# In front of the MLP: eight modulation steps instead of six, and the first quarter's residual rows made by ScalarE and GpSimd

## The chip, the core and the metric

The kernel runs on one core of one Trainium2 chip. The metric is the device time of one launch in microseconds (us); lower is better. The figure for a kernel is the median of its runs.

## What is computed

One step of one layer of a decoder trunk, for 256 prompt tokens and 8 sample tokens, with 2048 channels, all in float32. Only the part around the change matters here:

```
mod = silu(c) @ w_ada + b_ada                     # 2048 x (6*2048)
sh1, sc1, gt1, sh2, sc2, gt2 = split(mod, 6)
...                                               # three mixers -> merged
out = merged @ w_out
x   = x + gt1 * rmsnorm(out, g_post_mix)          # first residual
h2  = rmsnorm(x, g_pre_mlp) * (1 + sc2) + sh2
y2  = square(relu(h2 @ w_mlp_up)) @ w_mlp_down    # 2048 -> 8192 -> 2048
x   = x + gt2 * rmsnorm(y2, g_post_mlp)
```

## The kernel before, in words

Activations stand transposed: 128 channels in the partitions, 264 tokens (256 + 8) in the row. A weight block of 128x128 is stationary, the tokens move. Float32 accuracy is kept with three products per weight block: weights and activations are split into a high and a low part ("whi"/"wlo" for weights), and lines 671, 672 and 673 multiply high by high, high by low and low by high. A *granule* is 4x256 or 2x512 weights, read by one SyncE load into a "raw" buffer; ScalarE writes the high part (line 631), VectorE the low part (line 113). There are buffers for three granules of split weights, so the splits run up to three granules ahead of TensorE, and each split waits for TensorE to give a buffer back.

The output projection (`w_out`) is eight blocks of 256 channels, m = 0 to 7, four granules each. Behind each block `gated` makes the squares (line 1461) and the gated values g (VectorE line 1464, ScalarE line 1467), and adds the squares to `sqacc` (line 110). One granule into the next block, TensorE turns g round to token rows (line 893). Then `block_rows` takes products on VectorE (line 1482), copies the rows into the tiles `og` (ScalarE line 1489, VectorE line 1490) and takes squares on ScalarE (line 1486). g lies in a tile "gt", of which there are two; g of a block can be written only when the squares of the block two before it are through.

The last of the six modulation vectors (gt2) isn't needed until the end of the MLP. It is made in 16 *steps*, k = 0 to 15; a step loads two tiles of 128x1024 from `w_ada` (line 346) and does four matmuls (line 383). `pre.load` loads the first six steps during the output projection, and `rounds.steps(n)` puts n of them into TensorE's program at three places in front of the MLP: two behind the last block, one behind the transposes of the last g, three behind the sums for the sample tokens. The other ten are done inside the MLP, in five batches of two.

In front of the MLP stands a chain of small work. The row norm r1 comes out of `sqacc` (lines 1505, 1506 and 235 to 240); the norm r2 of the new x is worked out from sums without making the new x first (lines 1561 to 1581). Then `quad(q)` makes, for a quarter of the channels, x transposed and scaled by r2: a matmul of x1 with a diagonal matrix `dg` that holds r2 (line 1617). For the first quarter x1 isn't updated yet, so a second matmul adds og times a diagonal of r1*r2 (line 1619; `d1` holds r1). `put_quad` scales, shifts and splits the result (VectorE line 1629, ScalarE line 1631, splits at lines 113 and 116). `residual(q)` makes x1 + og*r1 for a quarter on VectorE (line 1597); `begin_up` runs the first 512 columns of the up projection with quads 1 to 3 and residuals 2, 3 and, last, 0 in between.

Tiles named `b` all come from one pool of 28 (`NBLK`): 128 partitions by 1056 floats. In the output projection these are the merged activations in two parts (8 tiles), x1 (4), og (4; the two for the second half of the channels are first written at block 4) and the loaded steps (2 each).

Who orders what: in the output projection only TensorE's order is the one written; a scheduler orders the other engines and gives out the tiles when the program is built. From `rounds.steps(2)` to the end of `begin_up` TensorE, VectorE and ScalarE have the written order. Every engine runs its list strictly in order.

Of the kernel before, what the change touches and what calls it, by code (L numbers as in the profile page):

```python
# [10 lines left out]
AF = mybir.ActivationFunctionType  # L11
ALU = mybir.AluOpType
# [3 lines left out]
P = 128  # L16
D = 2048
KT = D // P
# [25 lines left out]
RATES = ((1.8, 0.5), (1.6, 0.5), (1.25, 0.5), (1.0, 0.5))  # L44
ST_BUFS = 4
VB_BUFS = 2
N_PRE = 6
PRE_AT = (2, 3, 4)
ADA_BATCH = 4
ADA_LEAD = 3  # L50
PAIRED = 72
# [13 lines left out]
def hybrid_step_kernel(  # L65
# [9 lines left out]
    V, S, T = nc.vector, nc.scalar, nc.tensor  # L75
# [13 lines left out]
    def nm(s):  # L89
        uid[0] += 1  # L90
        return f"{s}_{uid[0]}"

    def blk(shape=None, dt=F32):
        shape = shape or [P, 4, NT]
        return blkp.tile(shape, dt, tag="b", name=nm("b"))

    def sm(shape=None):
        return psm.tile(shape or [P, 512], F32, tag="sm", name=nm("sm"))

    def tmp(shape, tag, bufs=2):  # L100
        return tp.tile(shape, F32, tag=tag, name=nm(tag), bufs=bufs)
# [17 lines left out]
    def apart(v):  # L119
        return v.rearrange("p n (r c) -> p n r c", r=2)  # L120

    def by_two(v):
        return v.rearrange("p n (c r) -> p n r c", r=2)
# [15 lines left out]
    ident, ones, triu = cst[:, 0:128], cst[:, 128:256], cst[:, 256:384]  # L139
# [91 lines left out]
    def rstd_sqrt(ms, scale, out):  # L231

        n, w = out.shape
        xx, aa = tmp([P, 16], "sx")[0:n, 0:w], tmp([P, 16], "sa")[0:n, 0:w]
        S.activation(out, ms, AF.Sqrt, scale=scale, bias=eps)
        V.tensor_scalar(xx, ms, scale, EPS, ALU.mult, ALU.add)
        V.reciprocal(out, out)
        mul(aa, out, out)
        V.scalar_tensor_tensor(aa, aa, -0.5, xx, ALU.mult, ALU.mult)
        V.scalar_tensor_tensor(out, aa, 1.5, out, ALU.add, ALU.mult)  # L240
# [154 lines left out]
    rounds = Rounds()  # L395
# [343 lines left out]
    def new_acc():  # L739
        return pmm.tile([P, 2, 512], F32, tag="mm", name=nm("mm"))  # L740

    def linear(w, k0, nk, c0, width, xh, xl):

        acc = new_acc()
        kc = min(nk, 1024 // width)
        for kb in range(0, nk, kc):
            granule(w, k0, kc, c0, width, [acc], xh, xl, kb, kb == 0, kb + kc == nk)
            background()
        return acc[:, 0:width // P, 0:NT]
# [698 lines left out]
    x1 = [[blk([P, 1024]) for _ in range(2)] for _ in range(2)]  # L1448
# [6 lines left out]
    def gated(m, src, Gv):  # L1455

        k = 2 * m
        sq = tmp([P, 2, NT], "vt")
        g = tmp([P, 2, NT], "gt")
        if m < 7:  # L1460
            S.activation(sq, src, AF.Square)
        else:
            S.activation(sq[:, 0, :], src[:, 0, :], AF.Square)
        V.tensor_scalar(g[:, 1, 0:NP], src[:, 1, 0:NP], Gv[:, k + 1, 0:1], None, ALU.mult)
        if m == 7:
            S.activation(sq[:, 1, :], src[:, 1, :], AF.Square)
        S.activation(g[:, 0, 0:NP], src[:, 0, 0:NP], AF.Copy, scale=Gv[:, k, 0:1])
        if m == 0:
            add(sqacc, sq[:, 0, :], sq[:, 1, :])
        else:  # L1470
            add(sqacc, sqacc, sq[:, 0, :])
            add(sqacc, sqacc, sq[:, 1, :])
        mul(gs[:, k:k + 2, :], src[:, :, NP:NT], Gv[:, k:k + 2, 1:NC])
        return g
# [17 lines left out]
    def block_rows(m, g):  # L1492

        pt = to_tokens(g)
        for t in range(2):
            products(m, t, g, pt)
        put_rows(m, pt, og)
        for t in range(2):
            squares(m, t, g, pt)

    def norms():

        ps = sm([P, 2 + NS])
        for t in range(2):
            T.matmul(ps[:, t:t + 1], sqacc[:, t * P:(t + 1) * P], ones[:, 0:1], start=True, stop=True)
        T.matmul(ps[:, 2:2 + NS], ones, sqacc[:, NP:NT], start=True, stop=True)
        r = tmp([P, 2 + NS], "nr", 1)
        rstd_sqrt(ps, 1.0 / D, r)
        return r
# [3 lines left out]
    og = [[blk([P, 1024]) for _ in range(2)] for _ in range(2)]  # L1513
# [3 lines left out]
    pre = Rounds()  # L1517
    pre.todo = [(5, k) for k in range(KT)]
    for m in range(8):
        if m in PRE_AT:  # L1520
            n = N_PRE // len(PRE_AT)
            for _ in range(n):
                pre.load(True)
        z = linear(w_out[0], 0, KT, m * CW, CW, mH, mL)
        if m < 7:
            g = gated(m, z, G1)
            later.append((now[0], lambda m=m, g=g: block_rows(m, g)))
        if m == 6:

            S.activation(tmp([P, 1], "srr", 1), sqacc[:, 0:1], AF.Sqrt)  # L1530
    rounds.drain()
    rounds = pre
# [4 lines left out]
    order = tc.manual_schedule(engines={mybir.EngineType.PE, mybir.EngineType.DVE, mybir.EngineType.Activation})  # L1537
    order.__enter__()
    Q = nc.gpsimd
    rounds.steps(2)  # L1540
    g = gated(7, z, G1)

    sp = tmp([P, 2, KT, NS], "os2", 1)
# [2 lines left out]
    r1 = norms()  # L1546
# [13 lines left out]
    both = tmp([P, 2, 2 + NS], "fs")  # L1560
    V.reduce_sum(both[:, :, 2:2 + NS], ps.rearrange("p s k b -> p s b k"), axis=mybir.AxisListType.X)
    V.reduce_sum(both[:, :, 0:2], sums, axis=mybir.AxisListType.X)
    rounds.steps(3)

    d1 = tmp([P, 2, P], "vt")
    for t in range(2):
        S.activation(d1[:, t, :], ident, AF.Copy, scale=r1[:, t:t + 1])
    for t in range(2):
        S.copy(in_rows(og, t, 7), pt[:, t])

    xa = tmp([P, KT, NS], "xsn", 1)
    Q.tensor_tensor(gs, gs, r1[:, 2:2 + NS].unsqueeze(1).to_broadcast([P, KT, NS]), op=ALU.mult)
    Q.tensor_tensor(xsT, xsT, gs, op=ALU.add)
    Q.tensor_tensor(xa, xsT, A2[:, :, 1:NC], op=ALU.mult)

    q = tmp([P, 2 + NS], "rr", 1)
# [4 lines left out]
    V.tensor_scalar(q, q, 0.0, None, ALU.max)  # L1581
    r2 = tmp([P, 2 + NS], "rr0", 1)
    rstd_sqrt(q, 1.0 / D, r2)
    dg = tmp([P, 4, P], "gt")
    for t in range(2):
        V.tensor_scalar(dg[:, t, :], ident, r2[:, t:t + 1], None, ALU.mult)
        S.activation(dg[:, 2 + t, :], d1[:, t, :], AF.Copy, scale=r2[:, t:t + 1])
    Q.tensor_tensor(xa, xa, r2[:, 2:2 + NS].unsqueeze(1).to_broadcast([P, KT, NS]), op=ALU.mult)
    Q.tensor_tensor(xa, xa, B2[:, :, 1:NC], op=ALU.add)
    h2h, h2l = [blk(dt=F32R) for _ in range(4)], [blk(dt=F32R) for _ in range(4)]  # L1590
# [1 line left out]
    def residual(q):  # L1592

        cs = slice(q % 2 * 512, q % 2 * 512 + 512)
        for t in range(2):
            x = x1[t][q // 2][:, cs]
            V.scalar_tensor_tensor(x, og[t][q // 2][:, cs], r1[:, t:t + 1], x, ALU.mult, ALU.add)

    def quad(q):

        hs, ls = (apart(h[q])[:, :, :, NP // 2:NT // 2] for h in (h2h, h2l))
        xq = by_two(xa[:, 4 * q:4 * q + 4, :])
        Q.tensor_copy(hs, xq)
        Q.tensor_tensor(ls, xq, hs.bitcast(F32), op=ALU.subtract)
        for i2 in range(2):
            if q > 0:
                ps = sm([P, 2, NP])
            vt = tmp([P, 2, NT], "vt")
            for i in range(2):
                c0 = q % 2 * 512 + (2 * i2 + i) * P  # L1610
                if q == 0:
                    pk = sm([P, NP])
                else:
                    pk = ps[:, i, :]
                for t in range(2):
                    o = pk[:, t * P:(t + 1) * P]
                    T.matmul(o, x1[t][q // 2][:, c0:c0 + P], dg[:, t, :], start=True, stop=q > 0)  # L1617
                    if q == 0:
                        T.matmul(o, og[t][0][:, c0:c0 + P], dg[:, 2 + t, :], start=False, stop=True)
                if q == 0:  # L1620
                    put_quad(q, i2, i, pk, vt)
            if q > 0:
                for i in range(2):
                    put_quad(q, i2, i, ps[:, i, :], vt)

    def put_quad(q, i2, i, src, vt):
        k = 4 * q + 2 * i2 + i
        if i == 0 and (q == 0 or i2 == 0):
            V.tensor_scalar(vt[:, i, 0:NP], src, A2[:, k, 0:1], B2[:, k, 0:1], ALU.mult, ALU.add)
        else:  # L1630
            S.activation(vt[:, i, 0:NP], src, AF.Identity, scale=A2[:, k, 0:1], bias=B2[:, k, 0:1])
        if q == 0 or i == 1:
            a = i if q == 0 else 0
            js = slice(2 * i2 + a, 2 * i2 + i + 1)
            split_tokens(vt[:, a:i + 1, 0:NP], h2h[q][:, js, :], h2l[q][:, js, :], 0, NP)

    quad(0)
    residual(1)

# [5 lines left out]
    def begin_up():  # L1645

        accs = [new_acc(), new_acc()]
        for k in range(0, KT, 2):
            granule(w_mlp_up[0], 0, 2, 0, 2 * CW, accs, h2H, h2L, k, k == 0, k + 2 == KT)
            if k % 4 == 0 and k + 4 < KT:  # L1650
                quad(k // 4 + 1)
            elif k + 6 < KT:
                residual(k // 4 + 2)
            elif k + 2 == KT:
                residual(0)
            if k >= 8:
                background()
        return [a[:, :, 0:NT] for a in accs]
# [107 lines left out]
    dg = tmp([P, 2, P], "vt")  # L1766
# [81 lines left out]
```

## Time and profile before

| | |
|---|---|
| median of 3 runs | 1822.57 us (1820.84 to 1825.6) |
| the profiled execution's own time | 1821.44 us |
| its span, first to last instruction | 1819.4 us |
| its mean granted TensorE clock | 0.998 |
| busy: TensorE, VectorE, ScalarE, GpSimd | 98%, 65%, 55%, 8% |
| HBM traffic over the span | 241 GB/s |

Times in the profile are us from the span's start. A group's row gives busy time and mean length; a timeline row gives start, length, engine, line, operation and, in brackets, how long the engine stood idle ahead of it and what ended that. TensorE's matmul rows overlap: a matmul's row is longer than the distance to the next one. The output projection's last block begins at about 1070 us; the MLP's first granule starts at 1093.92 us.

### The profile page before, as it was taken

What the parts mean: (1) busy time and instruction counts of PE and PEld (TensorE: products, weight loads), DVE (VectorE), ACT (ScalarE), POOL (GpSimd) and SP (SyncE); (2) the same over time, 40 slices, a digit from 0 to 9 for tenths busy, and PEclk for the clock granted to TensorE, in tenths of its full rate; (3) what the DMA queues carried; (4) which work ended last, traced back from release to release, by engine and by line L of the source; (5) the groups of instructions that cost most, each with busy time, mean ns of one, the idle gap of its engine ahead of it and who ended that gap; (6) DMA issues with size and microseconds to landing.
All of it is one profiled execution on the core that took longest, in us unless ns stands there. A gap on an engine that the chain in (4) does not pass through costs nothing.

```text
span 1819.4 us, 42092 instructions
## 1 busy us (share of the span) xinstructions
PE 1780.7 (98%) x16970; PEld 1690.5 (93%) x16970; DVE 1179.1 (65%) x2077; ACT 997.2 (55%) x1824; POOL 138.3 (8%) x228
## 2 busy tenths in 40 slices
PE   7999999999999999999999999999999999999998
PEld 5889999989989988989999989999999999999998
DVE  5566668787576686566555667555666666666666
ACT  5344454666756756655445666454554545454544
POOL 4222000111111111210000000000000000000000
PEclk9999999999999999999999999999999999999999
DMA  9997587788788788897978954877666666666663
GB/s 325 379 347 282 196 293 247 218 260 295 230 285 262 228 261 302 274 326 241 305 252 267 330 166 153 251 255 222 196 195 193 196 196 195 198 196 194 195 193 118
DMA packets 330179, 442.05 MB, mean 243 GB/s; under 512 B 14946, under 2 KB 276944, under 8 KB 329984
## 3 DMA queue, kind: packets, MB, share of 16 engines
q1 hardware_dynamic: 311872, 380.52, 64.7%
q0 software_dynamic: 17184, 57.85, 8.9%
q8 instruction: 133, 2.18, 0.5%
q10 hardware_dynamic: 928, 0.99, 0.2%
q14 instruction: 62, 0.51, 0.1%
HBM read 427.60 MB, written 11.70 MB: 241 GB/s over the span
## 4 chain that ended last, share of the span: by engine, by line
PE 83%; issue 3%; DVE 3%; DMA 3%; ACT 1%; POOL 0%; ACTq 0%; DVEq 0%; SPq 0%; POOLq 0%
PE mm L671 25%; PE mm L673 25%; PE mm L672 25%; PE ada L383 3%; DMA vbc<-vs_d 2%; DVE wlo L113 1%; PE ada L315 1%; PE sm L893 1%; DMA raw<-in_w_in_dram 1%; DVE b L113 1%; PE sm L712 0%; ACT whi L631 0%; PE sm L705 0%; DMA araw<-in_w_ada_dram 0%; PE sm L1617 0%
## 5 line engine op out<-in xcount | busy, mean ns | idle before, releaser
L671 PE MATMUL mm<-b,whi 128*128 128x264 f32 x4600 | 1284.5, 279 | 7.5 <-ACT b L116 3.9
L673 PE MATMUL mm<-b,wlo 128*128 128x264 f32 x4600 | 1272.5, 277 | 6.4 <-DVE wlo L113 4.9
L672 PE MATMUL mm<-b,whi 128*128 128x264 f32 x4600 | 1271.3, 276 | 0.7 <-DVE b L113 0.7
L113 DVE TENSOR_TENSOR wlo<-raw,whi 128x512 fp32r<-128x512 f32 x1136 | 768.8, 689 | 430.4 <-ACT whi L631 427.0
L631 ACT CAST whi<-raw 128x512 fp32r<-128x512 f32 x1136 | 689.0, 616 | 628.9 <-DVE wlo L113 318.9
L671 PEld LDWEIGHTS mm<-b,whi 128*128 128x128 f32 x4600 | 870.8, 189 | 48.2 <-issue 24.8
L673 PEld LDWEIGHTS mm<-b,wlo 128*128 128x128 f32 x4600 | 870.8, 189 | 8.6 <-DVE wlo L113 7.0
L672 PEld LDWEIGHTS mm<-b,whi 128*128 128x128 f32 x4600 | 871.1, 189 | 1.3 <-DVE b L113 1.1
L110 DVE TENSOR_TENSOR b<-b,mm 128x528 f32<-128x528 f32 (+1 forms) x137 | 95.6, 699 | 73.4 <-PE mm L673 65.8
L1148 DVE SCALAR_TENSOR_TENSOR st<-vbc,b,st 128x128 f32<-128x128 f32 (+1 forms) x96 | 34.2, 391 | 54.8 <-DMA vbc<-vs_d 49.9
L1146 ACT ACTIVATE st<-st,fs 128x128 f32<-128x128 f32 (+1 forms) x96 | 37.2, 431 | 51.7 <-DMA st<-in_state_hgrn_dram 29.5
L1785 POOL TENSOR_TENSOR gs<-b,G 128x16 f32<-128x16 f32 x1 | 0.2, 222 | 714.1 <-DVE b L110 714.1
L502 POOL DMA_DIRECT2D b<-in_w_ada_dram x64 | 46.3, 726 | 38.4 <-PE ada L315 31.6
L383 PE MATMUL ada<-araw,cT 128*32 128x512 f32 x296 | 40.8, 601 | 0.4 <-DMA araw<-in_w_ada_dram 0.4
L315 PE MATMUL ada<-b,cT 128*32 128x256 f32 (+1 forms) x640 | 35.2, 358 | 2.1 <-DMA b<-in_w_ada_dram 1.9
L107 DVE TENSOR_TENSOR b<-b,b 128x512 f32<-128x512 f32 (+1 forms) x47 | 34.0, 743 | 1.3 <-ACT b L1260 1.1
L1149 POOL DMA_DIRECT2D out_dram<-st x32 | 23.5, 736 | 132.0 <-DVE st L1148 132.0
L315 PEld LDWEIGHTS ada<-b,cT 128*32 128x32 f32 x640 | 18.2, 114 | 14.2 <-DMA b<-in_w_ada_dram 5.6
L383 PE MATMUL ada<-b,cT 128*32 128x512 f32 x216 | 26.2, 593 | 0.0
L113 DVE TENSOR_TENSOR b<-gt,b 128x528 fp32r<-128x528 f32 x32 | 22.8, 712 | 3.2
L113 DVE TENSOR_TENSOR b<-b 128x1024 f32<-128x1024 f32 (+1 forms) x24 | 24.4, 1019 | 0.0
L1671 ACT ACTIVATE b<-vt 128x528 fp32r<-128x528 f32 x32 | 22.9, 714 | 1.0
(366 smaller groups left out, 902.4 us busy)
## 6 DMA issues: line engine op xcount, KB each, us to landing
raw<-in_w_in_dram SPq DMA_DIRECT2D x231, 512.0 KB, 5.0
raw<-in_w_mlp_up_dram SPq DMA_DIRECT2D x128, 512.0 KB, 3.9
raw<-in_w_mlp_down_dram SPq DMA_DIRECT2D x128, 512.0 KB, 3.6
araw<-in_w_ada_dram SPq DMA_DIRECT2D x74, 512.0 KB, 5.7
b<-in_w_ada_dram SPq DMA_DIRECT2D x54, 512.0 KB, 6.4
b<-in_w_ada_dram POOLq DMA_DIRECT2D x48, 512.0 KB, 10.4
raw<-in_w_branch_dram SPq DMA_DIRECT2D x48, 512.0 KB, 4.5
raw<-in_w_out_dram SPq DMA_DIRECT2D x32, 512.0 KB, 4.9
```

Source lines behind the costliest of these rows:

```text
L107: V.tensor_tensor(o, a, b, op=ALU.mult)
L110: V.tensor_tensor(o, a, b, op=ALU.add)
L113: V.tensor_tensor(o, a, b, op=ALU.subtract)
L315: T.matmul(acc[32 * j:32 * j + 32, 0:n], cT[:, k, :], w[:, n * j:n * j + n], start=k == 0, stop=k == KT - 1)
L383: T.matmul(self.acc[32 * j:32 * j + 32, :], cT[:, k, :], ws[j // 2][:, j % 2 * 512:j % 2 * 512 + 512], start=k == 0, stop=k == KT - 1)
L502: queue.dma_start(w[:, i], w1[k * P:(k + 1) * P, :, self.k0 * P:(self.k0 + self.n) * P])
L631: S.copy(hi, raw)
L671: T.matmul(o, a, xh(k + j), start=first and j == 0, stop=False)
L672: T.matmul(o, a, xl(k + j), start=False, stop=False)
L673: T.matmul(o, b, xh(k + j), start=False, stop=last and j == n - 1)
L1146: S.activation(st[:, i, :], st[:, i, :], AF.Copy, scale=fs[:, h0 + i, b:b + 1])
L1148: V.scalar_tensor_tensor(st[:, i, :], v[:, i, :], k[:, h0 + i, NP + b:NP + b + 1], st[:, i, :], ALU.mult, ALU.add)
```

## The change

Eight steps are loaded ahead instead of six: one during block 1, two each during blocks 2 and 3, three during block 4. The one of block 1 goes into the two "araw" buffers, the other seven take 14 tiles of the pool instead of 12. In front of the MLP they stand as 3 + 1 + 4 instead of 2 + 1 + 3. The first quarter of x1 is updated before quad(0): ScalarE writes og*r1 into a tile `ou`, one instruction of 128x512 for each of the two token tiles, and GpSimd adds it to x1. quad(0) then needs one product per tile and row half, like the other quads; `d1`, the second pair of diagonals and the last `residual(0)` go.

```diff
-N_PRE = 6
-PRE_AT = (2, 3, 4)
+PRE_AT = {1: 1, 2: 2, 3: 2, 4: 3}
...
     for m in range(8):
-        if m in PRE_AT:
-            n = N_PRE // len(PRE_AT)
-            for _ in range(n):
-                pre.load(True)
+        for i in range(PRE_AT.get(m, 0)):
+            pre.load(m > 1)
         z = linear(w_out[0], 0, KT, m * CW, CW, mH, mL)
...
-    rounds.steps(2)
+    rounds.steps(3)
     g = gated(7, z, G1)
...
-    rounds.steps(3)
-
-    d1 = tmp([P, 2, P], "vt")
+    rounds.steps(4)
+
+    ou = blk([P, 2, 512])
     for t in range(2):
-        S.activation(d1[:, t, :], ident, AF.Copy, scale=r1[:, t:t + 1])
+        S.activation(ou[:, t, :], og[t][0][:, 0:512], AF.Copy, scale=r1[:, t:t + 1])
     for t in range(2):
         S.copy(in_rows(og, t, 7), pt[:, t])
...
     Q.tensor_tensor(gs, gs, r1[:, 2:2 + NS].unsqueeze(1).to_broadcast([P, KT, NS]), op=ALU.mult)
+    for t in range(2):
+        Q.tensor_tensor(x1[t][0][:, 0:512], x1[t][0][:, 0:512], ou[:, t, :], op=ALU.add)
     Q.tensor_tensor(xsT, xsT, gs, op=ALU.add)
...
-    dg = tmp([P, 4, P], "gt")
-    for t in range(2):
-        V.tensor_scalar(dg[:, t, :], ident, r2[:, t:t + 1], None, ALU.mult)
-        S.activation(dg[:, 2 + t, :], d1[:, t, :], AF.Copy, scale=r2[:, t:t + 1])
+    dg = tmp([P, 2, P], "gt")
+    V.tensor_scalar(dg[:, 0, :], ident, r2[:, 0:1], None, ALU.mult)
+    S.activation(dg[:, 1, :], ident, AF.Copy, scale=r2[:, 1:2])
...
                 for t in range(2):
                     o = pk[:, t * P:(t + 1) * P]
-                    T.matmul(o, x1[t][q // 2][:, c0:c0 + P], dg[:, t, :], start=True, stop=q > 0)
-                    if q == 0:
-                        T.matmul(o, og[t][0][:, c0:c0 + P], dg[:, 2 + t, :], start=False, stop=True)
+                    T.matmul(o, x1[t][q // 2][:, c0:c0 + P], dg[:, t, :], start=True, stop=True)
...
-            elif k + 2 == KT:
-                residual(0)
```

How the built program moves. In the changed kernel line numbers are one lower up to the output projection (382 for 383, 892 for 893) and up to four lower behind it.

**TensorE, one granule into the last block (m = 7), before.** "sm" is the PSUM tile that takes block 6's g turned round; "mm" is the accumulator of block 7.

```order
L673 MATMUL mm_14769<-b_12299,wlo_14686 128x264
L893 MATMUL sm_14804<-cst,gt_14760 128x128 x4
L671 MATMUL mm_14769<-b_12735,whi_14715 128x264
L672 MATMUL mm_14769<-b_12736,whi_14715 128x264
L673 MATMUL mm_14769<-b_12735,wlo_14716 128x264
```

The same place now; "ada" is the accumulator of the modulation steps, and each pair of rows is one step:

```order
L672 MATMUL mm_14777<-b_12299,wlo_14694 128x264
L382 MATMUL ada_14930<-araw_13807,cT 32x512 x2
L382 MATMUL ada_14930<-araw_13809,cT 32x512 x2
L382 MATMUL ada_14930<-b_13967,cT 32x512 x2
L382 MATMUL ada_14930<-b_13969,cT 32x512 x2
L382 MATMUL ada_14930<-b_13971,cT 32x512 x2
L382 MATMUL ada_14930<-b_13973,cT 32x512 x2
L892 MATMUL sm_14812<-cst,gt_14768 128x128 x4
L670 MATMUL mm_14777<-b_12735,whi_14723 128x264
```

The three steps that are written behind block 7 stand three granules earlier, in front of the transposes of block 6.

**ScalarE over the same stretch, before**, from block 6's squares on, with what each instruction waits for:

```order
L1461 ACTIVATE vt_14759<-mm_14611 128x528 [waits PE_49]
L631 CAST whi_14794<-raw_14689 128x512 [waits DMAHW1_49,PE_49]
L1467 ACTIVATE gt_14760<-mm_14611,G_13644 128x256 [waits DVE_49]
L631 CAST whi_14798<-raw_14689 128x512 [waits PE_49]
L1530 ACT_TABLE_LOAD
L1530 ACTIVATE srr_14767<-a_2234_13654 128x1 [waits DVE_49]
L631 CAST whi_14839<-raw_14723 128x512 [waits DMAHW2_49,PE_49,Activation_49]
L1489 COPY b_13659<-sm_14804 128x256 [waits DVE_49]
L631 CAST whi_14843<-raw_14723 128x512 [waits PE_49,Activation_49]
L1486 ACTIVATE gt_14760,fs_13662<-sm_14804 128x256 [waits DVE_49]
L1486 ACTIVATE gt_14760,fs_13662<-sm_14804 128x256 [waits Activation_49]
```

And now (b_13659 is og's tile for the first 128 tokens and the second half of the channels; sm_14498 and sm_14654 are the turned rows of blocks 4 and 5, gt_14768 is block 6's g):

```order
L1460 ACTIVATE vt_14767<-mm_14619 128x528 [waits PE_49]
L630 CAST whi_14802<-raw_14697 128x512 [waits DMAHW3_49,DVE_49,PE_49]
L1527 ACT_TABLE_LOAD
L1527 ACTIVATE srr_14775<-a_2234_13654 128x1 [waits DVE_49]
L1488 COPY b_13659<-sm_14498 128x256 [waits PE_49]
L1488 COPY b_13659<-sm_14654 128x256
L630 CAST whi_14806<-raw_14697 128x512 [waits Activation_49]
L1485 ACTIVATE gt_14456,fs_13662<-sm_14498 128x256 [waits DVE_49]
L1485 ACTIVATE gt_14612,fs_13662<-sm_14654 128x256 [waits DVE_49]
L1485 ACTIVATE gt_14456,fs_13662<-sm_14498 128x256 [waits Activation_49]
L1485 ACTIVATE gt_14612,fs_13662<-sm_14654 128x256 [waits Activation_49]
L1466 ACTIVATE gt_14768<-mm_14619,G_13644 128x256 [waits DVE_49]
```

Row copies and squares of blocks 4 and 5, which stood in their own blocks, now stand in a heap ahead of block 6's g, and the first of them waits for TensorE.

**GpSimd in front of the MLP, now.** b_13646 and b_13648 are x1's first halves, b_15002 is `ou`, xsn the sample tokens' h2, rr the norm r2:

```order
L1569 TENSOR_TENSOR gs_13655<-gs_13655,nr_14959 128x128 [waits DVE_49,Pool_49]
L1572 TENSOR_TENSOR xsT<-xsT,gs_13655 128x128 [waits Pool_49]
L1573 TENSOR_TENSOR xsn_15007<-xsT,A_14925 128x128 [waits Pool_49]
L1571 TENSOR_TENSOR b_13646<-b_13646,b_15002 128x512 [waits DMASW1_49,Activation_49]
L1571 TENSOR_TENSOR b_13648<-b_13648,b_15002 128x512 [waits DMASW3_49,Activation_49]
L1586 TENSOR_TENSOR xsn_15007<-xsn_15007,rr_2461_15019 128x128 [waits DVE_49,Pool_49]
```

The two rows of line 1571 are new; the others stood in this order before.

## The prediction

> **What bounds the kernel now.** I read the page first, then the waits and the timeline around the seam between output projection and MLP, then the chain of waits there.
>
> ```profile
> PE 83%; issue 3%; DVE 3%; DMA 3%; ACT 1%; POOL 0%; ACTq 0%; DVEq 0%; SPq 0%; POOLq 0%
> 1080.00:1100.00 20.00, 18.24 (x151) 12.83 (x151) 12.85 (x40) 10.25 (x27) 4.99 (x15) 1.00 0.23 63
> ```
>
> The chain that ends last is TensorE's for 83% of the span: what TensorE does or waits for costs time, what others do costs only where TensorE waits. The second row is a stretch of 20 us around the seam (busy time of TensorE, its weight loads, VectorE, ScalarE, GpSimd, then clock, DMA share, GB/s). TensorE's 18.24 contain the modulation steps that are put there as filling:
>
> ```profile
> 1072.64 0.60 PE L893 MATMUL sm<-cst,gt 128*128 128x128 f32 x4
> 1081.27 1.92 PE L383 MATMUL ada<-b,cT 128*32 128x512 f32 x16
> 1083.95 0.61 PE L1505 MATMUL sm<-cst,a 128*128 128x1 f32 x4 [0.75 <-DVE a L110]
> 1086.83 2.78 PE L383 MATMUL ada<-b,cT 128*32 128x512 f32 x24
> 1090.36 0.46 PE L1617 MATMUL sm<-gt,b 128*128 128x128 f32 x2 [0.75 <-PE ada L383]
> ```
>
> Two steps fill the wait behind the last block and leave 0.75 us of it; three fill the wait for r2 and leave 0.75 us. A third step costs 2.78 - 1.92 = 0.86 us, so one more in each place would overrun by 0.1 us at most. That is the plan one reads in the diff. Why the waits are there, the chain of waits shows:
>
> ```profile
> 1081.27 0.63 ACT whi L631
> 1081.91 0.69 DVE wlo L113
> 1082.61 0.41 DVE gt L1464
> 1083.46 0.45 DVE a L110
> 1091.53 0.56 DVE vt L1629
> 1096.24 1.30 DVE b L1597 x2
> ```
>
> From the last block's end (1081.2) to 1083.95 one split, g and the sums run one after the other; from 1091.53 to 1097.5 the splits of the first quarter and `residual(1)` do. Neither gets shorter by what TensorE does meanwhile.
>
> **The change, part by part.**
>
> *The heap in block 7.* The pool has 28 tiles: 8 activations, 4 x1, 4 og and 12 for six steps fill it exactly. Now it is 14, and two of og's tiles, first written at block 4, have to wait for a step to give its tiles back. That is what the order shows: row copies and squares of blocks 4 and 5 stand in a heap behind a wait for TensorE, block 6's g behind the heap, TensorE's transposes (line 892) behind g, and three steps ahead of them. Its price goes by these rows:
>
> ```profile
> 1075.92 0.62 ACT L631 CAST whi<-raw 128x512 fp32r<-128x512 f32 x1 [0.28 <-PE mm L672]
> 1076.46 0.38 ACT L1486 ACTIVATE gt<-sm 128x256 f32<-128x256 f32 x1
> 1076.97 0.38 ACT L1486 ACTIVATE gt<-sm 128x256 f32<-128x256 f32 x1
> 1077.34 0.61 ACT L631 CAST whi<-raw 128x512 fp32r<-128x512 f32 x1
> 1087.31 0.65 ACT L1569 COPY b<-mm 128x256 f32<-128x256 f32 x2 [0.38 <-DVE gt L1482]
> 1071.90 0.47 ACT L1467 ACTIVATE gt<-mm,G 128x256 f32<-128x256 f32 x1
> ```
>
> The steps start where the transposes stood, at 1072.64. The first step has the araw tiles; the second is the first to free pool tiles, and two steps take 1.92: 1074.56. Then ScalarE makes two copies (0.65), one split (1076.46 - 1075.92 = 0.54), four squares (0.51 from one to the next, 0.37 behind the last: 3 x 0.51 + 0.37 = 1.90) and g (0.47): 3.56 together, 1078.12. VectorE's half of g must come first, into the same tile, which the third square sets free; I add 0.2 for that and the hand-overs and take 1078.3. The transposes come 1078.3 - 1072.64 = **5.66 us later**, and TensorE stands idle for 5.66 - 2.78 = 2.9 of these. Bounds: 4.6 if the copy's wait ends before ScalarE reaches it (about 1073.5), 6.5 if it is for the third step. Block 7's other granules have their splits in stock, so no second wait is added, and the wait behind block 7 has the same length as before but nothing to fill it.
>
> *The clock.* Idle TensorE can lose its clock:
>
> ```profile
> 394.27:397.68 3.41, 1.76 (x13) 1.00 0.33 124
> 397.68:401.09 3.41, 3.41 (x18) 0.50 0.93 303
> 797.04:800.46 3.42, 1.84 (x16) 1.00 0.66 224
> 800.46:803.87 3.41, 3.41 (x34) 1.00 0.96 287
> ```
>
> These are windows of 3.41 us (busy TensorE, clock, DMA). After one with 1.76 us busy the next had half the clock and 18 matmuls instead of 34; after one with 1.84 us it had not. So some 1.6 us of idle time in one window costs the next up to 1.7 us. A wait of 2.9 us misses that only if it is cut nearly in half by a window's edge; the wait behind block 7, 2.75 us now unfilled, is a second chance. I take **+1.4 us** (0 to 3.4, both waits). [...]
>
> *GpSimd's adds and the r2 chain.* Their length and what they hold up:
>
> ```profile
> 1087.22 0.43 POOL L1574 TENSOR_TENSOR xsn<-xsT,A 128x128 f32<-128x128 f32 x1
> 1092.38 0.25 POOL L1604 TENSOR_TENSOR b<-xsn,b 128x32 fp32r<-128x32 f32 x1
> 1087.73 0.17 DVE L107 TENSOR_TENSOR rr<-fs,nr 128x10 f32<-128x10 f32 x1
> 1810.19 0.93 POOL L1787 TENSOR_TENSOR gs<-gs,nr 128x128 f32<-128x128 f32 x1 [2.50 <-DVE nr L240]
> 1810.75 0.92 DVE L1777 SCALAR_TENSOR_TENSOR b<-b,nr,b 128x512 f32<-128x512 f32 x1
> 1813.12 0.74 DVE L1777 SCALAR_TENSOR_TENSOR b<-b,nr,b 128x512 f32<-128x512 f32 x1
> ```
>
> (0.43 - 0.25)/96 is 1.9 ns an element, so 512 take 0.43 + 384 x 0.0019 = 1.16 us. Two from 1087.7 on end at 1090.1, ahead of the 1090.36 at which dg is there: alone they cost nothing. But just then VectorE works out r2 (line 107 at 1087.73 and what follows), from two operands in SBUF. The last three rows show that such instructions and GpSimd's get in each other's way: 0.93 instead of 0.43 us on GpSimd, 0.92 instead of 0.74 on VectorE, 0.18 for 128 elements. Four times as wide that is 0.72 for each add: r2, and with it quad(0), comes **1.44 us later**. The fourth step in that wait ends at 1086.83 + 2.78 + 0.86 = 1090.47 and hides behind it. Bounds: 0.1 (no contention, the fourth step alone) and 4.9 (each add at 0.93/128 x 512 = 3.7 us, ending at 1095.2). I take the row nearest in kind, the two-operand VectorE one. [...]
>
> *ScalarE's side.* Two `ou` instructions (0.54 apiece, by the spacing of the 512-wide split above) replace two short ones:
>
> ```profile
> 1086.25 0.68 ACT L1567 ACTIVATE vt<-cst,nr 128x128 f32<-128x128 f32 x2
> 1088.77 0.31 ACT L235 ACTIVATE rr<-rr,eps 128x10 f32<-128x10 f32 x1 [0.81 <-DVE rr L1581]
> ```
>
> ScalarE is 0.4 to 0.5 us later at the copies; the 0.81 it waits for r2's root hides that. Without the cover it would cost those 0.5.
>
> *Fewer products.* The first psum tile of quad(0) needs two products instead of four: 2 x 0.22 (1617 and 1619 alternate at 0.22 in the chain):
>
> ```profile
> 1090.82 0.22 PE sm L1619 x2
> 1091.04 0.22 PE sm L1617 x2
> ```
>
> The split chain starts **0.45 us earlier** and sets the rest until 1097.5; the other six products saved lie beside it and give nothing. `residual(0)` frees 1.3 us of VectorE behind the seam, where TensorE waits for nobody: 0.
>
> *One batch less in the MLP.*
>
> ```profile
> 1141.83 0.28 PE L673 MATMUL mm<-b,wlo 128*128 128x264 f32 x1
> 1142.04 1.07 PE L383 MATMUL ada<-araw,cT 128*32 128x512 f32 x8
> 1143.89 0.38 PE L671 MATMUL mm<-b,whi 128*128 128x264 f32 x1
> ```
>
> 1143.89 - 1141.83 less one matmul (0.11) is **1.95 us** saved, in full, since TensorE is never idle there. The loads moved forward pass SyncE's queue during blocks 1 and 4, ahead of later `w_out` loads; splits in stock cover that (0 to 1 us).
>
> Sum: 5.66 + 1.4 + 1.44 - 0.45 - 1.95 = **+6.1 us**. The profiled execution took 1821.44, so 1827.5 in its terms; it lies 1.1 below the median shown, and against that, 1822.57, it is **1828.7 us**.
>
> **The rivals.**
>
> *The clock stays full* (idle windows count only when wholly idle, or a window's edge cuts the wait in half). For: the row at 797.04. Against: the row at 394.27, and 2.9 us is longer than either. 4.7 us: 1827.3. Chance 0.15.
>
> *VectorE's ten-element instructions slip between GpSimd's reads.* For: they are short, and the first may start before the first add. Against: the 0.92. 6.1 - 1.44 + 0.1 = +4.8: 1827.3. Chance 0.2.
>
> *Not slower by a measurable amount: the copy waits for older work, not for a step's tile.* The order doesn't say which TensorE instruction is waited for. Then the heap starts at 1073.5, the transposes come 4.6 us late, TensorE idles 1.8 us, too little to lose the clock in most phases: 4.6 + 1.44 - 0.45 - 1.95 = +3.6: 1826.2. It decides if g of block 6 ends before 1077.3. Against: 30 tiles in a pool of 28. Chance 0.1.
>
> *GpSimd becomes the bound.* Each add 3.7 us, x1 ready at 1095.2, 4.9 instead of 1.44: +9.5, 1832.1. For: the 0.93. Against: VectorE's instructions there are short, at 1810 they were 0.74 each. Chance 0.1.
>
> *The steps are free, as planned* (no heap): -0.45 + 0.18 - 1.95 = -2.2, 1820.4. Against: the order. Chance 0.05.
>
> **How the numbers follow.** The forecast keeps 0.4. A measurement of this kernel tells about 0.3% from no change, 5.5 us: 1828.04 is the edge, and the forecast lies just beyond it. Slower by more: 0.32 from the forecast, 0.1 from GpSimd, and a third of the first two rivals (a second loss of clock, a later release), 0.12: 0.54. Faster by more: hardly a case, 0.04. Within: 0.42. The range goes from 1824.0 (no contention, no clock loss: +3.4 in the profiled execution's terms is 1824.9) to 1833.0 (GpSimd as the bound, or both waits losing the clock with the port locked whole).
>
> **What would show it.** Right: three steps at about 1072.6, TensorE idle for nearly 3 us ahead of line 892, ScalarE's copies of blocks 4 and 5 right behind each other, an unfilled 2.7 us ahead of line 1504, half the clock in one window behind; r2's VectorE chain with two holes while line 1571 runs; four batches in the MLP. Wrong: line 892 less than 4 us later against its block, or adds of over 2 us.

## The result and the profile after

The changed kernel takes 1825.69 us (median of 21 runs, 1822.4 to 1832.03), the kernel before, beside it, 1821.74 us (21 runs). The ratio is 1.0025, with a 95% interval of 1.0017 to 1.0034: slower by 3.1 to 6.2 us. The prediction had +6.1 us and 1828.7; the time lies in its range, and the sign is right. But 0.25% is less than the 0.3% that the prediction drew as its line, so what came is "within" (chance 0.42) and not "slower by more" (0.54).

The profiled execution of the changed kernel has a span of 1823.8 us against 1819.4, 4.4 more; 0.40 us of that stood already at the end of block 7's first granule, 0.31 of it from the moved loads (see below the table of pieces). First the waits of TensorE from 1066 to 1112 us, after (who waits for whom: us in all, times, the longest):

```profile
PE sm L1504 <- DVE a L109: 2.6, 1, 2.6
PE sm L1615 <- DVE gt L1584: 2.1, 1, 2.1
PE sm L892 <- ACT gt L1466: 1.2, 1, 1.2
PE sm L1615 <- DVE b L1595: 0.2, 1, 0.2
```

Before there were two waits of 0.75. Now there are 2.6 behind the last block (its three steps have left it), 2.1 in front of quad(0), although a fourth step stands there, and 1.2 ahead of block 6's transposes. The timeline after, one granule into block 7:

```profile
1072.42 1.28 ACT L1527 ACT_TABLE_LOAD   x1
1073.14 1.06 PE L382 MATMUL ada<-araw,cT 128*32 128x512 f32 x8
1073.71 0.20 ACT L1527 ACTIVATE srr<-a 128x1 f32<-128x1 f32 x1
1073.82 0.63 ACT L1488 COPY b<-sm 128x256 f32<-128x256 f32 x2
1074.21 0.76 DVE L1489 COPY b<-sm 128x256 f32<-128x256 f32 x2 [1.02 <-PE ada L382]
1074.86 0.40 ACT L1485 ACTIVATE gt<-sm 128x256 f32<-128x256 f32 x1
1075.23 0.39 ACT L1485 ACTIVATE gt<-sm 128x256 f32<-128x256 f32 x1
...
1076.11 0.48 DVE L1463 TENSOR_SCALAR gt<-mm,G 128x256 f32<-128x256 f32 x1 [0.42 <-ACT gt L1485]
1076.63 0.47 ACT L1466 ACTIVATE gt<-mm,G 128x256 f32<-128x256 f32 x1 [0.19 <-DVE gt L1463]
...
1077.15 0.66 PE L892 MATMUL sm<-cst,gt 128*128 128x128 f32 x4 [1.24 <-ACT gt L1466]
```

The heap is there, and the steps stand ahead of the transposes; ScalarE ran its rows in the order built, from the table load at 1072.42 to g at 1076.63. But ScalarE's copies begin right behind the table load and `srr`, with no idle time ahead of them, while the first step is still running. The bracket of VectorE's copies names a step (1.02 us), but it is inferred from the times: in the built program VectorE's first copy waits for ScalarE's first copy, which ends at the same moment (1074.18). The squares are 0.36 to 0.37 us apart. The timeline after, in front of the MLP:

```profile
1088.52 0.61 PE L1504 MATMUL sm<-cst,a 128*128 128x1 f32 x4 [2.61 <-DVE a L109]
...
1091.40 3.64 PE L382 MATMUL ada<-b,cT 128*32 128x512 f32 x32
...
1092.19 2.52 POOL L1571 TENSOR_TENSOR b<-b,b 128x512 f32<-128x512 f32 x2
1092.32 1.18 DVE L106 TENSOR_TENSOR rr<-fs,nr 128x10 f32<-128x10 f32 x1
1093.53 1.20 DVE L1577 SCALAR_TENSOR_TENSOR rr<-fs,rr 128x10 f32<-128x10 f32 x1
1094.77 0.17 DVE L106 TENSOR_TENSOR rr<-rr,nr 128x10 f32<-128x10 f32 x1
...
1097.13 0.57 PE L1615 MATMUL sm<-gt,b 128*128 128x128 f32 x3 [2.09 <-DVE gt L1584]
```

The two adds take about 1.26 us each. Two VectorE instructions of ten elements, 0.17 us each before, take 1.18 and 1.20, one for each add; the second ends as the adds end, at 1094.7. That is 2.04 us, and the wait of 2.09 in front of quad(0) is its trace.

The batches in the MLP, as groups of TensorE's step products from 1100 us on (before, then after; shortest, median and longest in ns, first and last start; eight of an "araw" group make a batch):

```profile
L383 PE MATMUL ada<-araw,cT x40: 592/605/617, 1142.0 to 1258.7; 128*32 128x512 f32 x40
```

```profile
L382 PE MATMUL ada<-araw,cT x32: 592/605/617, 1148.3 to 1236.0; 128*32 128x512 f32 x32
```

Five batches became four.

All kernels can be laid side by side at the seam, in four pieces taken from the starts of TensorE's matmuls: (a) from the last matmul of block 7's first granule to the transposes of block 6's g, (b) from there to the sums for r1 (line 1505 before), (c) from there to quad(0), (d) from there to the granule behind quad(1). Full times differ by some us between executions for reasons outside the seam (1817.55 to 1825.6 in the 21 runs of the kernel before); these pieces agree within a few hundredths wherever two kernels do the same. The kernels e1 to e7 are the experiments below.

| | a | b | c | d | sum | against before, with the batch |
|---|---|---|---|---|---|---|
| before | 0.11 | 11.31 | 6.41 | 8.81 | 26.64 | 0 |
| after | 4.22 | 11.37 | 8.61 | 8.37 | 32.57 | +5.93 - 1.95 = +3.98 |
| e1, steps alone | 4.23 | 11.37 | 6.45 | 8.86 | 30.91 | +4.27 - 1.95 = +2.32 |
| e2, adds alone | 0.11 | 11.31 | 8.60 | 8.37 | 28.39 | +1.75 |
| e3, no shortage | 0.11 | 11.35 | 8.61 | 8.35 | 28.42 | +1.78 - 1.95 = -0.17 |
| e4, no shortage, no adds' half | 0.11 | 11.35 | 6.45 | 8.84 | 26.75 | +0.11 - 1.95 = -1.84 |
| e5, adds in pieces | 0.11 | 11.35 | 7.84 | 8.38 | 27.68 | +1.04 - 1.95 = -0.91 |
| e6, 4 + 1 + 3 steps | 4.22 | 11.37 | 9.23 | 8.37 | 33.19 | +6.55 - 1.95 = +4.60 |
| e7, adds left out | 0.12 | 11.34 | 6.45 | 8.40 | 26.31 | -0.33 - 1.95 = -2.28 |

Piece a is the heap, c holds r2's chain, d the splits of the first quarter. The last column takes 1.95 for the batch from the prediction. The traces give 2.07: from the granule behind quad(1) to TensorE's last matmul the two kernels with five batches take 714.50 and 714.51 us, the seven with four 712.42 to 712.45. That would move each value with "- 1.95" down by 0.12.

The pieces begin in block 7; ahead of them the moved loads cost something too. From block 0's transposes to those of block 5 the kernel before takes 56.20 us, the changed kernel 56.51 and e1 56.72; the other six are within 0.01 of before. In the three kernels with the shortage (after, e1, e6) SyncE issues the loads of two steps in one go in block 4 (four instead of two, at 1035.52 us after), and a split of block 5 comes 1.0 to 1.5 us late, waiting for its weights. In e1:

```profile
1046.33 1.14 ACT L630 CAST whi<-raw 128x512 fp32r<-128x512 f32 x2 [2.27 <-DMA raw<-in_w_out_dram]
```

Behind that, block 4's g is late, and TensorE waits 0.31 us for it in e1 and 0.10 after; in e6 the delay just fits. (This is read from the traces; no run changes it alone.) After against before is thus 0.31 + 5.93 - 2.07 = +4.17 by the traces, and +4.55 by the ratio (1821.74 x 0.0025): they tell the same.

### The profile page after: what moved, and what is told of

Its sections match the earlier page's. It is cut to its first block, busy times and chain, and to the rows that moved or that the text cites. A ratio compares the mean times of both kernels' runs of the same rounds, so it can differ in the third digit from the quotient of the medians.

```text
span 1823.8 us, 42066 instructions
## 1 busy us (share of the span) xinstructions
PE 1781.2 (98%) x16954; PEld 1690.7 (93%) x16954; DVE 1180.8 (65%) x2074; ACT 997.5 (55%) x1823; POOL 140.9 (8%) x230
## 4 chain that ended last, share of the span: by engine, by line
PE 87%; DVE 3%; ACT 1%; issue 1%; DMA 1%; POOL 0%; ACTq 0%; DVEq 0%; SPq 0%
PE mm L670 27%; PE mm L672 26%; PE mm L671 26%; PE ada L382 3%; DVE wlo L112 1%; PE ada L314 1%; DMA vbc<-vs_d 1%; PE sm L892 1%; PE sm L704 1%; PE sm L711 0%; DVE b L112 0%; PE sm L1615 0%; DMA araw<-in_w_ada_dram 0%; ACT whi L630 0%; DVE b L106 0%
```

## Experiments

**e1: the steps alone.** The kernel before with eight steps, 3 + 1 + 4.

```diff
-N_PRE = 6
-PRE_AT = (2, 3, 4)
+PRE_AT = {1: 1, 2: 2, 3: 2, 4: 3}
-    rounds.steps(2)
+    rounds.steps(3)
-    rounds.steps(3)
+    rounds.steps(4)
```

> The kernel before with the eight steps alone (loads, 3 + 1 + 4 places); the first quarter keeps its two products and GpSimd makes no adds. If the pool's shortage is what the steps bring: the transposes stand again behind three steps and ScalarE's heap, 4.1 us late, the fourth step in the wait for r2 adds 0.1, the missing batch takes 1.95 off: 2.2 us slower than before, and r2's VectorE instructions take 0.17 each again. If the seam's loss comes from GpSimd's adds alone and the steps are free as the diff plans: 1.8 us faster than before. If the lost clock window counts (TensorE's 2.1 us wait for r2 is gone here, so the window behind it should be whole): still 2.2, and no half window near 1098; 1.7 less would have to be missing otherwise.

Measured: ratio to before 1.0020 (1.0008 to 1.0033), 1.5 to 6.0 us slower; by the pieces 2.32. The waits of TensorE at the seam:

```profile
PE sm L1504 <- DVE a L109: 2.6, 1, 2.6
PE sm L892 <- ACT gt L1466: 1.2, 1, 1.2
PE sm L1614 <- DVE b L1594: 0.3, 2, 0.2
```

The heap and the unfilled wait behind block 7 come with the steps, as expected to a tenth; the wait for r2 does not: the four steps fill it. The clock stayed whole through the seam (1.00 in every stretch from 1076.94 to 1100.83).

**e2: the adds alone.** The other half, with six steps as 2 + 1 + 3.

```diff
-PRE_AT = {1: 1, 2: 2, 3: 2, 4: 3}
+N_PRE = 6
+PRE_AT = (2, 3, 4)
-    rounds.steps(3)
+    rounds.steps(2)
-    rounds.steps(4)
+    rounds.steps(3)
```

> The kernel before with the other half alone: og*r1 by ScalarE, GpSimd's two adds, one product per tile and row half; six steps in their old places 2 + 1 + 3. No shortage, no heap: the transposes stand where they stood. If an add locks VectorE out for its whole length: two of r2's instructions take about 1.2 us instead of 0.17, TensorE waits about 2.8 us in front of quad(0) instead of 0.75, and with 0.45 saved on the products the kernel is 1.6 us slower than before. By the price on record (0.72 for each add): 1.0 slower. If VectorE slips between GpSimd's reads: 0.4 faster. A wait of 2.8 us may cost the clock of the next window; quad(0)'s splits run there and set the pace, so nothing of it should be seen in the end.

Measured: ratio 1.0001 (0.9989 to 1.0013), which leaves room for anything from 2.0 us faster to 2.4 slower; the time alone decides nothing. The pieces give +1.75: c is 2.19 longer, d 0.44 shorter. VectorE there:

```profile
1083.12 1.19 DVE L107 TENSOR_TENSOR rr<-fs,nr 128x10 f32<-128x10 f32 x1
1084.34 1.19 DVE L1580 SCALAR_TENSOR_TENSOR rr<-fs,rr 128x10 f32<-128x10 f32 x1
1085.57 0.17 DVE L107 TENSOR_TENSOR rr<-rr,nr 128x10 f32<-128x10 f32 x1
```

The same two holds of 1.2 us without any shortage or heap. The wait in front of quad(0), 2.9 us here, cost no window of the clock (1.00 in every stretch from 1083.76 to 1094.00).

**e3: eight steps without a shortage.** The changed kernel whole, but the eighth step lies in four buffers that are idle by then.

```diff
-            for i in range(2):
+            for i in range(4 if place == "st" else 2):
+                if place == "st":
+                    w = tmp([P, 4, P], "st", ST_BUFS).rearrange("p a b -> p (a b)")
...
-            pre.load(m > 1)
+            pre.load("st" if (m, i) == (4, 2) else m > 1)
```

> The changed kernel whole, but the eighth step lies in four 128x512 buffers of the recurrent states, which are idle by then, so that the pool's 28 tiles suffice. If the shortage is the cause: no heap, block 6's transposes one granule into block 7 with no step ahead of them, three steps behind block 7 that overrun their wait by 0.1 us, four in the wait for r2; 4.0 us faster than the changed kernel, which is 0.1 to 0.3 us below before (2.05 - 0.45 + 0.1 - 1.95 = -0.25). If the steps' number or place costs the 4.1 us (their loads in front of w_out's, three steps at once), nothing is gained against the changed kernel: 4.3 slower than before.

Measured: ratio 0.9995 (0.9984 to 1.0006); by the pieces -0.17, where -0.25 was expected. The timeline behind block 7, and the one long wait of TensorE at the seam:

```profile
1081.98 1.06 PE L388 MATMUL ada<-araw,cT 128*32 128x512 f32 x8
1082.86 1.90 PE L388 MATMUL ada<-b,cT 128*32 128x512 f32 x16
1084.69 0.61 PE L1510 MATMUL sm<-cst,a 128*128 128x1 f32 x4
```

```profile
PE sm L1621 <- DVE gt L1590: 2.1, 1, 2.1
```

The three steps are behind block 7 again and fill the wait there to the end. Piece a is 0.11 as before. So it is two missing tiles, and not the number of steps, that made the heap: 4.11 us.

**e4: the same eight steps, with the first quarter as before.** e1 with the loading of e3, which is this edit in e1:

```diff
-            pre.load(m > 1)
+            pre.load("st" if (m, i) == (4, 2) else m > 1)
```

> The same eight steps without a shortage, and the first quarter as before (two products, no GpSimd adds). With heap and lock both gone only the plan of the diff is left: 0.1 us overrun behind block 7, 0.1 in front of quad(0), 1.95 saved in the MLP: 1.75 us faster than before, the fastest of all. If something else in the eight steps costs (loads that make TensorE wait for splits in blocks 1 to 4, up to 1 us): 0.8 faster. If the 1.95 of the batch is not saved in full: no change.

Measured: ratio 0.9987 (0.9976 to 0.9997), 0.5 to 4.4 us faster than before; by the pieces 1.84. It is the fastest of the complete kernels: faster than the kernel before and than the changed one. TensorE's only waits at the seam:

```profile
PE sm L1620 <- DVE b L1600: 0.3, 2, 0.2
```

The plan that the prediction read in the diff holds when it has room: one step more in each wait costs 0.04 in each (pieces b and c), and the batch saves 1.95.

**e5: the adds in pieces.** e3, each add cut into four.

```diff
-        Q.tensor_tensor(x1[t][0][:, 0:512], x1[t][0][:, 0:512], ou[:, t, :], op=ALU.add)
+        for j in range(4):
+            js = slice(j * P, j * P + P)
+            Q.tensor_tensor(x1[t][0][:, js], x1[t][0][:, js], ou[:, t, js], op=ALU.add)
```

> As e3 (no shortage), with each of GpSimd's adds cut into four of 128x128; one such instruction took 0.43 us before. If VectorE is locked out for one whole GpSimd instruction: no instruction of r2's chain is held for more than one piece, so none takes over 0.6 us, where two took 1.2 each in e2 and e3; the holds spread over more of the ten, some 0.2 to 0.3 each, and r2 is late by 1.0 to 2.2 us again. If the hold goes by the amount read (the 0.18 us for 128 elements of the prediction): four of the chain's instructions at 0.35, 1.4 late in all. [...]

Measured (one profile): GpSimd and VectorE in front of quad(0):

```profile
1089.34 3.36 POOL L1579 TENSOR_TENSOR b<-b,b 128x128 f32<-128x128 f32 x8
1089.46 0.36 DVE L106 TENSOR_TENSOR rr<-fs,nr 128x10 f32<-128x10 f32 x1
1089.86 0.38 DVE L1585 SCALAR_TENSOR_TENSOR rr<-fs,rr 128x10 f32<-128x10 f32 x1
1090.28 0.38 DVE L106 TENSOR_TENSOR rr<-rr,nr 128x10 f32<-128x10 f32 x1
1090.69 0.38 DVE L109 TENSOR_TENSOR rr<-rr,xx 128x10 f32<-128x10 f32 x1
1091.11 0.38 DVE L1588 TENSOR_SCALAR rr<-rr 128x10 f32<-128x10 f32 x1
1091.53 0.38 DVE L235 TENSOR_SCALAR sx<-rr 128x10 f32<-128x10 f32 x1
1091.86 0.22 DVE L236 RECIPROCAL rr<-rr 128x10 f32<-128x10 f32 x1
...
1092.35 0.38 DVE L238 SCALAR_TENSOR_TENSOR sa<-sa,sx 128x10 f32<-128x10 f32 x1
```

A piece starts every 0.42 us, and so do VectorE's first six instructions: the two engines take turns, one whole instruction each. No hold is longer than a piece, and seven instructions are held for 0.2 us each; the reciprocal between them takes 0.22 as it does without adds. The hold did not go by what is read: the same elements cost r2 1.39 us here (c 7.84 against 6.45 in e7) and 2.16 in e3. The total alone would not tell this apart from the second case, which had 1.4; the number of instructions held does, seven at 0.38 instead of four at 0.35.

**e6: four steps ahead of the transposes.** The changed kernel with 4 + 1 + 3.

```diff
-    rounds.steps(3)
+    rounds.steps(4)
-    rounds.steps(4)
+    rounds.steps(3)
```

> The changed kernel with its eight steps as 4 + 1 + 3: the shortage stays, and four steps instead of three stand ahead of block 6's transposes. If ScalarE's heap alone sets when the transposes can go: they start 4.1 us behind their place again, TensorE waits 0.4 instead of 1.24 us ahead of them, and one step less lies in the wait for r2, which is 0.86 longer. If the steps set it (a tile of the last one is waited for): 4.9 us behind their place, with the 1.24 us of waiting unchanged.

Measured (one profile): piece a is 4.22, the same to a hundredth as with three steps, and TensorE's wait ahead of the transposes is 0.38 instead of 1.24:

```profile
1073.23 0.20 ACT L1527 ACTIVATE srr<-a 128x1 f32<-128x1 f32 x1
1073.34 0.63 ACT L1488 COPY b<-sm 128x256 f32<-128x256 f32 x2
...
1076.14 0.47 ACT L1466 ACTIVATE gt<-mm,G 128x256 f32<-128x256 f32 x1 [0.19 <-DVE gt L1463]
...
1076.67 0.66 PE L892 MATMUL sm<-cst,gt 128*128 128x128 f32 x4 [0.38 <-ACT gt L1466]
```

ScalarE's heap alone sets when the transposes go. (Why the built order has the steps ahead of them stays open.) What was not expected stands behind block 7. These are stretches of 3.41 us, with busy time of TensorE, its weight loads, VectorE, ScalarE and GpSimd, then the clock, DMA share and GB/s:

```profile
1084.88:1088.29 3.41, 0.80 (x7) 0.61 (x7) 2.43 (x6) 1.66 (x4) 0.12 (x1) 1.00 0.72 173
1088.29:1091.70 3.41, 3.41 (x18) 1.76 (x17) 1.14 (x6) 1.59 (x6) 1.60 (x4) 0.50 0.41 139
1091.70:1095.12 3.42, 3.42 (x18) 1.09 (x18) 2.19 (x10) 1.39 (x4) 2.89 (x3) 0.50 0.00 0
```

The 2.61 us of waiting fell into one stretch, and the clock was halved through the next two, over the sums and the step products that r2's chain waits for. So VectorE comes to r2 late, when the first add is over and the second under way; it is held once, to the end of that add (1094.63). Piece c is 0.62 longer than after's:

```profile
1092.13 2.50 POOL L1571 TENSOR_TENSOR b<-b,b 128x512 f32<-128x512 f32 x2
1093.31 0.43 DVE L1558 TENSOR_REDUCE fs<-sm 128x16 f32<-128x256 f32 x1 [1.05 <-PE sm L1552]
...
1093.86 0.80 DVE L106 TENSOR_TENSOR rr<-fs,nr 128x10 f32<-128x10 f32 x1
1094.69 0.17 DVE L1577 SCALAR_TENSOR_TENSOR rr<-fs,rr 128x10 f32<-128x10 f32 x1
```

**e7: the adds left out.** e3 without the two GpSimd instructions.

```diff
-    for t in range(2):
-        Q.tensor_tensor(x1[t][0][:, 0:512], x1[t][0][:, 0:512], ou[:, t, :], op=ALU.add)
```

> As e3 (no shortage), and GpSimd's two adds are left out, so that the first quarter lacks og*r1 in the MLP's input and in the result. If the lock is all that the adds cost: no r2 instruction over 0.25 us, the four steps fill the wait for r2 but for 0.1, and from block 7's first granule to the granule behind quad(1) it takes 1.7 us less than in e3 (28.42), about 26.3 to 26.7. If ScalarE's two instructions of 128x512 also hold the chain up (r2's root stands behind them): 0.3 to 0.5 us of it stays.

Measured (one profile): c is 6.45 again and the sum 26.31, at the lower end of what was expected. The whole loss in c is what the adds hold up, 2.16 us with four steps filling the wait; ScalarE's two wide instructions leave nothing in it.

## Why the prediction was right in sign and too high

*The heap, +5.66: it came, but behind another release than predicted, and 1.5 us smaller.* Measured 4.11 in piece a (4.22 - 0.11; e1 4.12, and nothing in e3). The first step that failed is that og's two late tiles "have to wait for a step to give its tiles back". In the built program ScalarE's copy waits for the last product of block 7's first granule that reads b_12300, a tile of the merged activations, and og's b_13659 lies at the address where b_12300 lay (b_13661, VectorE's, where b_12299 lay). The activations of that granule are read there for the last time, so the two missing tiles came from them; no instruction of the heap waits for a step. The copy's wait and its tile's place are the same in e1 and e6. That granule was through at about 1073.2, 0.1 us into the first step. ScalarE got to the copies at 1073.8, because the table load of 1.28 us and `srr`, which stood behind block 6's g before, now stand ahead of it. So the copies began 0.68 us behind the first step's start (1073.82 against 1073.14), where "the second is the first to free pool tiles, and two steps take 1.92" put them at 1.92. This is the bound of 4.6 and the rival "the copy waits for older work", which got a chance of 0.1. The argument against it, 30 tiles in a pool of 28, says that somebody waits for a tile, not that the tile is a step's.

The second size that failed is the heap's length, 3.76 by the prediction (3.56 and 0.2 for hand-overs), 3.33 measured (1073.82 to 1077.15): four squares stood 0.36 apart, where 0.51 was taken from a pair of which the second waits for the first, since both write one tile (gt_14760); in the heap they alternate between two. (Against these 1.7 the steps themselves start 0.1 later than taken.) For the same reasons TensorE stood idle for 1.24, not 2.9.

*The clock, +1.4: nothing.* The wait on which the term mainly stood, 2.9 us ahead of the transposes, was 1.24 and too short. The wait behind block 7, 2.61, and the one for r2, 2.09, are longer than the 1.6 us of the prediction's estimate; the first was cut by a stretch's edge, and the second did lose the clock of the next:

```profile
1084.35:1087.76 3.41, 1.56 (x14) 1.37 (x13) 2.10 (x5) 1.68 (x4) 0.00 (x0) 1.00 0.72 223
1087.76:1091.17 3.41, 2.65 (x20) 1.55 (x20) 1.71 (x9) 2.07 (x8) 1.24 (x3) 1.00 0.53 157
...
1094.59:1098.00 3.41, 1.32 (x16) 0.90 (x9) 1.99 (x11) 0.70 (x2) 1.24 (x4) 1.00 0.00 0
1098.00:1101.42 3.42, 3.42 (x18) 3.42 (x17) 1.95 (x5) 2.01 (x5) 1.63 (x7) 0.50 0.00 0
```

It was lost at a place that the prediction didn't name, and there it is free: behind quad(0) VectorE's and ScalarE's splits and `residual(1)` set the pace. Piece d is 8.37 with half the clock, 8.37 in e2 with all of it (1.00 from 1087.18 to 1094.00) and 8.35 in e3 (mean clock 0.998 over the span, 0.997 after); in e2 and e3 TensorE waits 0.9 ahead of quad(1) instead. Lost behind block 7, as in e6, it costs: piece c is 0.62 longer there.

*The adds, +1.44: 2.20.* Piece c grew from 6.41 to 8.61, 0.04 of it for the fourth step. The step that failed is "four times as wide that is 0.72 for each add": the hold did not go by the amount read (1.39 us in e5 and 2.16 in e3 for the same elements). It went by how long the other engine's instruction still ran: VectorE's instructions end within 0.03 us of the add, after 1.18 and 1.20 us here, after 0.80 in e6, where one begins in the middle of an add. No run shows a port locked whole, which the upper end of the range names; what the runs show in its place is VectorE held until the add then under way ends, 1.18 to 1.21 us for 0.17 (after, e2, e3), and 2.16 us of piece c in all (e3 against e7).

*Fewer products, -0.45: -0.44* in d (-0.44 to -0.46 in the four kernels that have one product per tile and row half with the adds whole). *ScalarE's wider instructions, 0: 0* (e7). *One batch less, -1.95: -2.07.* *The moved loads, 0 to 1 us and put at 0: 0.31*, ahead of block 7.

Together +4.17 instead of +6.1: heap 1.5 too high, clock 1.4 too high, adds 0.76 too low, loads 0.3 too low, and the batch saved 0.1 more than taken. Two rivals came in their mechanism: the copy that waits for older work (+3.6) and, where it would have counted, the clock that stays full (+4.7). The sign rests on the heap, which was read from the order and came. That the sum lies in the range is in part luck: the adds were too low while heap and clock were too high. Of the signs that the prediction named, the three steps at about 1072.6, the copies in a row, the unfilled wait, the two holes and the four batches came; nearly 3 us of waiting ahead of line 892 and half the clock behind it did not. The two halves of the change are independent at the seam: e1's +4.27 and e2's +1.75 make 6.02, after has 5.93.

## What to carry to other kernels

When a change needs more buffers than a pool has, read from the order which engine's instruction waits for the release, then look up whose tile it gets and when that is read last, and whether the engine had anything left to wait for when it got there. Here the pool was two tiles short, the tiles came from the activations one granule into block 7, and what it cost was set by the work piled up behind, not by the wait. Before work is given to an idle GpSimd, look at what VectorE does at that time; here a chain of ten-element instructions paid up to 1.04 us of an add of about 1.26 each time it met one, and adds in four pieces held it up for 1.39 us in all instead of 2.16. Steps used as filling hide for almost nothing only where their buffers are free: idle buffers of an earlier phase turned 2.3 us of loss (e1) into 1.8 us of gain (e4, both by the pieces).

## What the runs showed of the hardware

*About half a stretch of idle TensorE went ahead of half the clock.* In each trace the half-clock stretches start multiples of 3.413 us apart (97 from 66.58 to 397.68 before, 205 from 398.27 to 1098.01 after), so that the stretches of a run can be laid out from any one of them. From 100 to 1810 us, in the nine traces, all nine stretches in which TensorE was idle for 1.99 us or more were followed by half the clock, none of the 19 with 1.2 to 1.64 us was, and of eleven with 1.65 to 1.92 us six were. So 1.65 us at 394.27 before, 1.84 at 394.86 after, 2.09 at 1094.59 after and 2.61 at 1084.88 in e6 were followed by a clock of 0.50; 1.58 at 797.04 before and 1.85 at 1084.35 after by one of 1.00. What decides in between stays open. In e6 a stretch without any idle time, 18 matmuls at half the clock (1088.29 to 1091.70), was itself followed by half the clock; why is open too.

*GpSimd and VectorE alternated by whole instructions* in r2's chain, with operands in SBUF: 0.17 us became 1.18 to 1.20 behind an add of about 1.26 us (after, e2), and 0.38 between pieces that start every 0.42 (e5). Held were instructions with two operands and, in e5, two `TENSOR_SCALAR` with one (0.38 for 0.17); the reciprocal was not held (0.22 with the pieces and without), and the product behind it hardly (0.20 for 0.17).
